# Another order of the experts' ranks in a mixture-of-experts layer, and each down projection loaded behind the next expert's gate and up

## The chip, the cores and the metric

The kernel runs on one core of a Trainium2 chip. The metric is the device time of one execution in microseconds (us); the median of several executions is compared.

## The reference

One decoder layer over 256 tokens of width 1024 in float32: a norm with modulation from a conditioning vector, a token mixer, and then a mixture of 64 experts, of which each token takes 8. The change touches the experts alone:

```python
def expert_block(args):
    x_b, g_b = args
    hg = jnp.einsum('td,edf->tef', x_b, w_gate)
    hu = jnp.einsum('td,edf->tef', x_b, w_up)
    return jnp.einsum('tef,efd->td', jax.nn.silu(hg) * hu * g_b[..., None], w_down)
```

`g_b` holds 8 gate values per token that aren't zero. `w_gate` and `w_up` are 1024 x 256 per expert and `w_down` is 256 x 1024, so each of the three matrices of an expert is 1 MiB.

## The kernel before

The first 260 us hold the norms, the token mixer, the router and a shared expert; the experts follow. At run time the experts are ranked by how many tokens they have. A unit is 32 tokens of one expert, and the table `UNITS` (line 32) fixes how many units each rank gets: 5 for ranks 0 and 1, 4 for rank 2, 3 for ranks 3 to 11, 2 for ranks 12 to 27, and 1 for ranks 28 to 48. `ORDER` (line 107) lists the ranks in the order in which they are worked. `plan_groups` (line 113) writes the units of the listed ranks one behind the other, after one unit for each of two experts loaded ahead of the ranking (ranks 64 and 65 in its lists), and cuts the list into 24 groups of 4 units, 128 token rows each. I number the groups from 0.

`run_groups` (line 1413) does a group in these steps, on TensorE in this order (helper `te`, line 1373, chains all of its matmuls, so they read L1378 in the profile): the gate and up products into the tile `pgu` (`pgum` in the profile), eight passes over the rows of the model width, and in each pass one matmul per part, a part being the neighbouring units that share an expert where `column_parts` (line 138) can merge them; the sums of the group before into `acc`; the gathering of token rows for later groups (`pgm`); transposes; and the down products (`pym`). In the first of the eight passes the matmul of each part needs its own expert's gate and up.

The weights arrive by transfers that SP issues from one queue, in program order. `load_experts` (line 1348) is called at the start of each group's code for the ranks that the group is the first to use. For each it takes the next pair of buffers from a ring of five (`wtiles`, line 1203; profile names gu, wbl, wbp for gate and up, and dn, wbs, wbd for down), reads the expert's number and issues gate, up and down, in this order:

```python
nc.sync.dma_start(out=gu[:, 0, :], in_=gsrc[ds(e * P, P), :], **kw)
nc.sync.dma_start(out=gu[:, 1, :], in_=usrc[ds(e * P, P), :], **kw)
late.append((dn, dsrc[ds(e * P, P), :], kw))
while late and not together:
    t, src, kw = late.pop()
    nc.sync.dma_start(out=t, in_=src, **kw)
```

A transfer into a buffer waits until TensorE has read what was in it for the last time, which was the expert five places earlier in the order; what is behind it in SP's queue waits too. In the last group (`together`) the down matrix is loaded in two halves by columns.

Of the kernel before, what the change touches and what calls it, by code (L numbers as in the profile page):

```python
# [17 lines left out]
SP = mybir.EngineType.SP  # L18

P = 128  # L20
T = 256
D = 1024
NE = 64
# [16 lines left out]
SKIPPABLE = 40  # L40
# [63 lines left out]

ORDER = [
    12, 0, 13, 28, 14, 29, 30, 15, 16, 3, 31, 17, 32, 33, 4, 34, 5, 35, 1, 18, 36, 19, 37, 38, 6, 39, 20, 21, 7, 40, 22, 41, 42,
    8, 43, 9, 44, 23, 24, 25, 45, 46, 10, 47, 11, 48, 26, 27, 2,
]  # L110


# [13 lines left out]
ULIST = [u for g in plan_groups() for u in g]  # L126
# [32 lines left out]
def tile_layer(ctx, tc, x, small, rows, w_ada, w_in, w_out, b_ada, gdn_norm_w, hg_norm_w, norm2_w, w_router, router_bias,  # L159
               w_gate, w_up, w_down, ws_gate, ws_up, ws_down, final_norm_w, consts, out, dbg=None):  # L160
# [999 lines left out]
    def glu(pgate, name):  # L1160

        sg = mo.tile([P, FE], F32, name=f"sg{name}", tag="sg", bufs=1)
        S.activation(sg, pgate[:, 0:FE], AF.Silu)  # L1163
        hh = mo.tile([P, 2, P], F32, name=f"hh{name}", tag="hh")
        V.tensor_tensor(hh.rearrange("p j q -> p q j"), sg.rearrange("p (q j) -> p q j", j=2),  # L1165
                        pgate[:, FE:2 * FE].rearrange("p (q j) -> p q j", j=2), op=ALU.mult)
        return hh
# [35 lines left out]
    def wtiles():  # L1203
        k = ring[0]
        ring[0] += 1
        return pairs[k % len(pairs)], downs[k % len(downs)]
# [138 lines left out]
    for b in range(2):  # L1345
        dense_down(hs[b], sdn, b, "sh", False)

    def load_experts(ranks, skippable, together):

        res, late = {}, []  # L1350
        for r in ranks:
            gu, dn = res[r] = wtiles()
            e = nc.values_load(order[0:1, r:r + 1], engines=[SP], min_val=0, max_val=NE - 1)
            kw = {}
            if skippable and r >= SKIPPABLE:
                n = nc.values_load(order[0:1, NE + r:NE + r + 1], engines=[SP], min_val=0, max_val=T)
                kw["cond"] = n > 0
            nc.sync.dma_start(out=gu[:, 0, :], in_=gsrc[ds(e * P, P), :], **kw)
            nc.sync.dma_start(out=gu[:, 1, :], in_=usrc[ds(e * P, P), :], **kw)
            late.append((dn, dsrc[ds(e * P, P), :], kw))  # L1360
            while late and not together:
                t, src, kw = late.pop()
                nc.sync.dma_start(out=t, in_=src, **kw)

        for n in range(2):
            for t, src, kw in late:
                t, src = (a.rearrange("p (j f) -> p j f", j=2)[:, :, n * 512:n * 512 + 512] for a in (t, src))
                nc.sync.dma_start(out=t, in_=src, **kw)
        return res

    last_pe = [None]

# [40 lines left out]
    def run_groups(u0, u1, prefix, skippable):  # L1413

        w = {NE + k: t for k, t in enumerate(ahead)}
        last_pe[0] = None
        groups = list(range(u0, u1, 4))
        starts = groups[::2]

        def batch(k):  # L1420
            return Batch(starts[k], min(8, u1 - starts[k]), f"{prefix}{starts[k]}")

        def scatter(n, st, yhl, name, first, stop):

            for k in range(2):
                for b in range(2):
                    te(TE.matmul, acc[b, n], lhsT=st[:, b, :], rhs=yhl[n][k], start=(first and k == 0), stop=(stop and k == 1), skip_group_check=True)

        before = None
        for k, u in enumerate(groups):  # L1430
            units = ULIST[u:u + 4]
            parts = column_parts([r for r, _ in units])
            name = f"{prefix}{u}"
            last = u + 4 == NMAIN
            new = [r for r in dict.fromkeys(r for r, _ in units) if r not in w]
            w.update(load_experts(new, skippable, last))
            if k == 0:
                nxt = batch(0)
                nxt.rows()
                for j2 in range(4):  # L1440
                    nxt.gather(j2)
            if k % 2 == 0:
                cur, nxt = nxt, None
                if k // 2 + 1 < len(starts):
                    nxt = batch(k // 2 + 1)
            o = P * (k % 2)
            if last:

                for n in range(2):
                    scatter(n, *before, False, True)  # L1450
                for n in range(2):
                    for b in range(2):
                        add_sums(b, n, name)

            pgu_ = pgu.tile([P, 512], F32, name=f"pgu{name}", tag="pgu")
            for j in range(8):
                for i, m, r in parts:
                    te(TE.matmul, pgu_[i:i + m, :], lhsT=cur.xg[j // 4][:, j % 4, o + i:o + i + m],
                       rhs=w[r][0][:, :, j * FE:j * FE + FE], start=(j == 0), stop=(j == 7))
            hh = glu(pgu_, name)  # L1460
            if before and not last:
                for n in range(2):
                    scatter(n, *before, not skippable and k == 1, False)

            ph = pht.tile([P, 512], F32, name=f"pht{name}", tag="pht")
            for b in range(2):
                te(TE.matmul, ph[:, 2 * P:2 * P + 8], lhsT=cur.sm[:, b, o:o + P], rhs=ghl[:, b, u // 4, :], start=(b == 0), stop=(b == 1))
            if nxt:
                if k % 2 == 0:
                    nxt.rows()  # L1470
                nxt.gather(2 * (k % 2))
            for j in range(2):
                te(TE.transpose, ph[:, j * P:j * P + P], hh[:, j, :], ident)
            hT_ = mo.tile([P, 2, P], F32, name=f"hTt{name}", tag="hTt")
            moved[0] = S.copy(hT_.rearrange("p j t -> p (j t)"), ph[:, 0:2 * P]).ins  # L1475
            gc = mo.tile([P, 1], F32, name=f"gc{name}", tag="gc")
            g4 = mo.tile([P, 8], F32, name=f"g4{name}", tag="g4")
            V.scalar_tensor_tensor(g4, ph[:, 2 * P:2 * P + 8], 1.0, blk4.rearrange("p k i -> p (k i)"), op0=ALU.mult, op1=ALU.mult, accum_out=gc)
            if nxt:
                nxt.gather(2 * (k % 2) + 1)  # L1480

            yhl = []
            for n in range(2):
                pyd = pg_.tile([P, 512], F32, name=f"py{name}{n}", tag="psg")
                for j in range(2):
                    for i, m, r in parts:
                        te(TE.matmul, pyd[i:i + m, :], lhsT=hT_[:, j, i:i + m],
                           rhs=w[r][1][:, j * D + n * 512:j * D + n * 512 + 512], start=(j == 0), stop=(j == 1))
                if last and n:
                    yh = mo.tile([P, 512], F32, name=f"yh{name}{n}", tag="yh")  # L1490
                    V.scalar_tensor_tensor(yh, pyd, gc, g2bc[:, n * 512:n * 512 + 512], op0=ALU.mult, op1=ALU.mult)
                    yhl.append((yh,))
                    continue
                yh, yl = (mo.tile([P, 512], F32R, name=f"y{c}{name}{n}", tag=f"y{c}") for c in "hl")
                if last:
                    y = mo.tile([P, 512], F32, name=f"y{name}{n}", tag="yd")
                    V.scalar_tensor_tensor(y, pyd, gc, g2bc[:, n * 512:n * 512 + 512], op0=ALU.mult, op1=ALU.mult)
                    S.copy(yh, y)
                    V.tensor_tensor(yl, y, yh.bitcast(F32), op=ALU.subtract)  # L1499
                else:  # L1500
                    S.activation(yh, pyd, AF.Copy, scale=gc)  # L1501
                    V.scalar_tensor_tensor(yl, pyd, gc, yh.bitcast(F32), op0=ALU.mult, op1=ALU.subtract)  # L1502
                yhl.append((yh, yl))
            before = cur.st[:, k % 2], yhl, name
        if not last:
            for n in range(2):
                scatter(n, *before, k == 0, True)
                for b in range(2):
                    add_sums(b, n, prefix)
            return  # L1510
        st, yhl, _ = before
        for n in range(2):
            sl = slice(n * 512, n * 512 + 512)
            for b in range(2):
                pso = acc[b, n]
                for k in range(2 - n):
                    te(TE.matmul, pso, lhsT=st[:, b, :].bitcast(F32) if n else st[:, b, :], rhs=yhl[n][k], start=(k == 0), stop=(k == 1 - n))
                V.tensor_tensor(x1[:, b, sl], x1[:, b, sl], pso, op=ALU.add)  # L1518
# [154 lines left out]
```

## Time and profile before

| | |
|---|---|
| median of 3 executions | 689.58 us (689.46 to 689.62) |
| the profiled execution, its own time | 688.26 us |
| span of its profile | 686.6 us |
| TensorE busy | 610.1 us, 89% of the span |
| VectorE / ScalarE / GpSimd busy | 301.3 / 209.6 / 121.7 us |
| bytes moved | 216.75 MB, mean 316 GB/s |
| mean granted TensorE clock | 0.953 |

The shares are means over stages. The expert stage is the stretch from about 260 us to 676 us; what a change there is worth has to be read from that stage's rows, and from what each engine waits for there.

### The profile page before, as it was taken

The page shows a single profiled execution, that of the slowest core. Times are in us where ns is not written, and L with a number is a line of the kernel's source. Part 1 is how long each engine was busy: PE and PEld are TensorE (multiplying, and loading weights), DVE is VectorE, ACT ScalarE, POOL GpSimd, SP SyncE. Part 2 cuts the span into 40 slices and gives each one's busy share as a digit, 9 for nine tenths or more (in the row PEclk, how much of TensorE's full clock was granted, in tenths as well). Part 3 has the DMA queues.
Part 4 walks back from the last instruction along what each step waited for, and adds up shares of the span by engine and source line. Part 5 has one row for each costly group of instructions (what it writes and reads, how often), then busy time and mean ns, then how long its engine had stood idle before and what let it go on. Part 6 is the DMA issues. An engine that isn't in the chain of part 4 may idle for free.

```text
span 686.6 us, 12745 instructions
## 1 busy us (share of the span) xinstructions
PE 610.1 (89%) x5161; PEld 379.2 (55%) x5162; DVE 301.3 (44%) x616; ACT 209.6 (31%) x410; POOL 121.7 (18%) x148
## 2 busy tenths in 40 slices
PE   4799887697889699999898899997998999799983
PEld 1499876586879687554443444543444444344441
DVE  4478999878998843122212022212121212121244
ACT  3356775433655321112111112111111111111113
POOL 7025273446566220000000000000000000000001
PEclk9899999889999879999999999998999999899998
DMA  8968383353665637796999999979999999999801
GB/s 350 421 275 313 138 330 127 125 200 156 262 243 217 263 137 298 314 376 244 408 426 420 422 422 422 423 259 420 424 422 424 420 425 420 425 416 425 348 0 66
DMA packets 31937, 216.75 MB, mean 316 GB/s; under 512 B 3760, under 2 KB 4096, under 8 KB 6400
## 3 DMA queue, kind: packets, MB, share of 16 engines
q1 hardware_dynamic: 31776, 215.83, 77.3%
q8 instruction: 42, 0.69, 0.4%
q14 instruction: 23, 0.19, 0.1%
q10 hardware_dynamic: 96, 0.04, 0.0%
HBM read 214.81 MB, written 1.05 MB: 314 GB/s over the span
## 4 chain that ended last, share of the span: by engine, by line
PE 61%; DMA 16%; DVE 16%; issue 3%; SPq 2%; ACT 2%; DVEq 0%; ACTq 0%
PE pgum L1378 21%; PE pym L1378 10%; PE acc L1378 6%; PE pgm L1378 5%; DMA wbl<-in_w_up_dram 5%; DMA gu<-in_w_up_dram 5%; DVE pacc L876 4%; PE pqk L437 3%; DMA ldA<-in_w_ada_dram 3%; PE pgs L1183 3%; DMA wbp<-in_w_up_dram 2%; DVE wps L451 2%; DVE cacc L541 2%; PE i L476 2%; PE gA L476 1%
## 5 line engine op out<-in xcount | busy, mean ns | idle before, releaser
L1378 PE MATMUL pgum<-wbl,xgm 128*32 128x512 f32 (+2 forms) x784 | 168.1, 629 | 6.6 <-DMA wbl<-in_w_up_dram 6.6
L1378 PE MATMUL pgum<-gu,xgm 128*32 128x512 f32 (+2 forms) x256 | 87.5, 606 | 7.5 <-DMA gu<-in_w_up_dram 7.5
L1378 PEld LDWEIGHTS pgum<-wbl,xgm 128*32 128x32 f32 (+2 forms) x784 | 47.5, 121 | 79.0 <-issue 79.0
L1165 DVE TENSOR_TENSOR hhm<-sgm,pgum 128x256 f32<-128x256 f32 x24 | 14.9, 621 | 172.1 <-ACT sgm L1163 172.1
L1378 PE MATMUL pgum<-wbp,xgm 128*32 128x512 f32 x224 | 78.0, 636 | 3.8 <-DMA wbp<-in_w_up_dram 3.8
L1536 POOL TENSOR_TENSOR o<-x_sb,fbc 128x512 f32<-128x512 f32 x2 | 2.5, 1269 | 418.1 <-DVE x_sb L1518 418.1
L1378 PE MATMUL pym<-wbs,hTtm 128*32 128x512 f32 (+1 forms) x272 | 72.6, 596 | 0.0
L1163 ACT ACTIVATE sgm<-pgum 128x256 f32<-128x256 f32 x24 | 9.2, 384 | 186.0 <-PE pgum L1378 186.0
L1502 DVE SCALAR_TENSOR_TENSOR ylm<-pym,gcm,yhm 128x512 fp32r<-128x512 f32 x46 | 34.6, 751 | 69.0 <-ACT yhm L1501 69.0
L1378 PE MATMUL pym<-wbd,hTtm 128*32 128x512 f32 (+2 forms) x232 | 61.7, 595 | 0.5 <-ACT hTtm L1475 0.5
L876 DVE SCALAR_TENSOR_TENSOR pacc<-ldc,cact,pacc 128x512 f32<-128x512 f32 x56 | 56.6, 1010 | 1.0
L1501 ACT ACTIVATE yhm<-pym,gcm 128x512 fp32r<-128x512 f32 x46 | 31.6, 687 | 76.1 <-PE pym L1378 76.1
L1378 PEld LDWEIGHTS pgum<-gu,xgm 128*32 128x32 f32 (+2 forms) x256 | 24.9, 126 | 46.0 <-issue 45.8
L1378 PE MATMUL pym<-dn,hTtm 128*32 128x512 f32 (+2 forms) x128 | 43.6, 596 | 0.5 <-ACT hTtm L1475 0.5
L1378 PE MATMUL pgm<-smm,h2hi 128*128 128x256 f32 x192 | 43.3, 305 | 0.0
L1378 PE MATMUL pgm<-smm,h2lo 128*128 128x256 f32 x192 | 38.5, 282 | 0.0
L1378 PE MATMUL acc<-yhm,stm 128*128 128x512 f32 x98 | 34.6, 434 | 0.0
L1378 PE MATMUL acc<-ylm,stm 128*128 128x512 f32 x94 | 29.8, 396 | 0.3 <-DVE ylm L1499 0.2
L1378 PEld LDWEIGHTS pgm<-smm,h2lo 128*128 128x128 f32 x192 | 29.6, 190 | 0.2 <-issue 0.2
L1378 PEld LDWEIGHTS pgm<-smm,h2hi 128*128 128x128 f32 x192 | 29.5, 190 | 0.3 <-issue 0.2
L1378 PEld LDWEIGHTS acc<-yhm,stm 128*128 128x128 f32 x98 | 16.7, 188 | 21.8 <-issue 18.9
L1378 PEld LDWEIGHTS pgum<-wbp,xgm 128*32 128x32 f32 x224 | 18.6, 116 | 16.3 <-issue 16.3
(454 smaller groups left out, 1082.4 us busy)
## 6 DMA issues: line engine op xcount, KB each, us to landing
wbl<-in_w_gate_dram SPq DMA_DIRECT2D x30, 1024.0 KB, 15.1
wbl<-in_w_up_dram SPq DMA_DIRECT2D x30, 1024.0 KB, 16.9
wbs<-in_w_down_dram SPq DMA_DIRECT2D x20, 1024.0 KB, 14.8
wbd<-in_w_down_dram SPq DMA_DIRECT2D x20, 1024.0 KB, 15.3
ldc<-in_w_ada_dram SPq DMA_DIRECT2D x16, 1024.0 KB, 7.9
gu<-in_w_gate_dram SPq DMA_DIRECT2D x11, 1024.0 KB, 15.1
gu<-in_w_up_dram SPq DMA_DIRECT2D x11, 1024.0 KB, 17.1
dn<-in_w_down_dram SPq DMA_DIRECT2D x10, 1024.0 KB, 15.4
```

The costliest lines, as they stand in the source:

```text
L437: TE.matmul(pqk[m // 2][:, (m % 2) * T:(m % 2) * T + T], lhsT=ws[j][PAIRS[k][0]][:, m * P:m * P + P], rhs=hT[:, PAIRS[k][1], j, :], start= ...
L451: engine(f"s_{key}{q}", "GGVG"[q]).tensor_tensor(lo, t[:, 2 * q:2 * q + 2, :], hi.bitcast(F32), op=ALU.subtract)
L476: TE.matmul(pj[:, i * T:i * T + T], lhsT=lh, rhs=rh, start=(i == 0 and j == 0 and k == 0), stop=(i == 1 and j == 7 and k == 2), skip_group ...
L541: V.scalar_tensor_tensor(acc, xp[:, k:k + T], convcol[:, 12 * k + blk:12 * k + blk + 1], acc, op0=ALU.mult, op1=ALU.add)
L876: engine(f"c{n}", "V").scalar_tensor_tensor(pa, t[:, :, j, :], cact[:, j:j + 1], pa, op0=ALU.mult, op1=ALU.add)
L1163: S.activation(sg, pgate[:, 0:FE], AF.Silu)
L1165: V.tensor_tensor(hh.rearrange("p j q -> p q j"), sg.rearrange("p (q j) -> p q j", j=2), pgate[:, FE:2 * FE].rearrange("p (q j) -> p q j", ...
L1183: TE.matmul(pg2[:, i * FE:i * FE + FE], lhsT=hT_all[j // 4][:, j % 4, b * P:b * P + P], rhs=gu[:, i, j * FE:j * FE + FE], start=(j == 0 an ...
L1378: last_pe[0] = fn(*args, **kw).ins
L1501: S.activation(yh, pyd, AF.Copy, scale=gc)
L1502: V.scalar_tensor_tensor(yl, pyd, gc, yh.bitcast(F32), op0=ALU.mult, op1=ALU.subtract)
L1536: G.tensor_tensor(o[b, n], x1[:, b, sl], fbc[:, sl], op=ALU.mult)
```

## The change

`ORDER` holds the same 49 ranks in another order, and the units of a rank stay together. `load_experts` becomes `load_gate`, which issues gate and up and puts the down load on the list `late`, and `load_downs(left)`, which issues from that list until `left` are on it. At the start of a group each new rank's gate and up is issued and then the downs but the newest one. After the group's gate and up products the gate and up of the first new rank of the next group are issued, and then the down that is left of this group. In the last group the downs of all ranks on the list come in halves at the end. Lines in the changed kernel stand one to eighteen lower.

```diff
 ORDER = [
-    12, 0, 13, 28, 14, 29, 30, 15, 16, 3, 31, 17, 32, 33, 4, 34, 5, 35, 1, 18, 36, 19, 37, 38, 6, 39, 20, 21, 7, 40, 22, 41, 42,
...
+    14, 12, 22, 19, 24, 15, 37, 11, 43, 13, 35, 18, 16, 6, 46, 8, 39, 4, 31, 10, 47, 1, 29, 23, 36, 38, 45, 0, 40, 32, 42, 7, 27,
...
-    def load_experts(ranks, skippable, together):
...
+    late = []
+
+    def load_gate(r, skippable):
+
+        gu, dn = wtiles()
+        e = nc.values_load(order[0:1, r:r + 1], engines=[SP], min_val=0, max_val=NE - 1)
...
+        nc.sync.dma_start(out=gu[:, 0, :], in_=gsrc[ds(e * P, P), :], **kw)
+        nc.sync.dma_start(out=gu[:, 1, :], in_=usrc[ds(e * P, P), :], **kw)
+        late.append((dn, dsrc[ds(e * P, P), :], kw))
+        return gu, dn
+
+    def load_downs(left, halves=False):
+
+        todo = [late.pop(0) for _ in range(max(len(late) - left, 0))]
+        if not halves:
+            for t, src, kw in todo:
                 nc.sync.dma_start(out=t, in_=src, **kw)
-
+            return
         for n in range(2):
-            for t, src, kw in late:
+            for t, src, kw in todo:
                 t, src = (a.rearrange("p (j f) -> p j f", j=2)[:, :, n * 512:n * 512 + 512] for a in (t, src))
                 nc.sync.dma_start(out=t, in_=src, **kw)
...
-            new = [r for r in dict.fromkeys(r for r, _ in units) if r not in w]
-            w.update(load_experts(new, skippable, last))
+            for r in dict.fromkeys(r for r, _ in units):
+                if r not in w:
+                    w[r] = load_gate(r, skippable)
+                    if not last:
+                        load_downs(1)
+            if last:
+                load_downs(0, True)
...
             hh = glu(pgu_, name)
+
+            ahead_ = 0
+            for r, _ in ULIST[u + 4:min(u + 8, u1)]:
+                if r not in w and not ahead_:
+                    w[r] = load_gate(r, skippable)
+                    ahead_ = 1
+            load_downs(ahead_)
```

From the two tables of ranks follow the groups. The number of ranks that each group, 0 to 23, is the first to use:

| | new ranks in groups 0 to 23 |
|---|---|
| before | 1 1 2 3 2 2 3 2 2 1 2 3 2 2 2 3 2 2 2 3 2 2 2 1 |
| changed | 1 2 2 3 2 2 2 2 2 2 2 1 3 2 2 2 2 2 2 2 2 2 2 3 |

Where the code moves instructions: SP's queue from the first expert loaded by rank, before. A name such as `wbl2` or `wbd0` is one buffer of the ring; only the transfers are shown.

```order
L1358 DMA wbp_2912<-in_w_gate_dram 128x2048
L1359 DMA wbp_2912<-in_w_up_dram 128x2048
...
L1363 DMA wbd0_2915<-in_w_down_dram 128x2048
...
L1358 DMA wbl2_2911<-in_w_gate_dram 128x2048
...
L1359 DMA wbl2_2911<-in_w_up_dram 128x2048
...
L1363 DMA wbd1_2916<-in_w_down_dram 128x2048
...
L1358 DMA wbl0_2909<-in_w_gate_dram 128x2048
...
L1359 DMA wbl0_2909<-in_w_up_dram 128x2048
...
L1363 DMA wbs0_2913<-in_w_down_dram 128x2048
...
L1358 DMA gu0_2704<-in_w_gate_dram 128x2048
```

The same place in the changed kernel:

```order
L1360 DMA wbp_2912<-in_w_gate_dram 128x2048
...
L1361 DMA wbp_2912<-in_w_up_dram 128x2048
...
L1360 DMA wbl2_2911<-in_w_gate_dram 128x2048
...
L1361 DMA wbl2_2911<-in_w_up_dram 128x2048
...
L1370 DMA wbd0_2915<-in_w_down_dram 128x2048
...
L1360 DMA wbl0_2909<-in_w_gate_dram 128x2048
...
L1361 DMA wbl0_2909<-in_w_up_dram 128x2048
...
L1370 DMA wbd1_2916<-in_w_down_dram 128x2048
...
L1360 DMA gu0_2704<-in_w_gate_dram 128x2048
...
L1361 DMA gu0_2704<-in_w_up_dram 128x2048
...
L1370 DMA wbs0_2913<-in_w_down_dram 128x2048
```

Each down has moved behind the gate and up of the next expert; the buffers go round the ring as before.

SP's queue at the end of the 24 groups, before:

```order
L1358 DMA wbl0_2909<-in_w_gate_dram 128x2048
...
L1359 DMA wbl0_2909<-in_w_up_dram 128x2048
...
L1363 DMA wbs0_2913<-in_w_down_dram 128x2048
...
L1358 DMA gu0_2704<-in_w_gate_dram 128x2048
...
L1359 DMA gu0_2704<-in_w_up_dram 128x2048
...
L1368 DMA dn0_2705<-in_w_down_dram 128x2x512
```

The same place in the changed kernel:

```order
L1360 DMA wbl0_2909<-in_w_gate_dram 128x2048
...
L1361 DMA wbl0_2909<-in_w_up_dram 128x2048
...
L1360 DMA gu0_2704<-in_w_gate_dram 128x2048
...
L1361 DMA gu0_2704<-in_w_up_dram 128x2048
...
L1375 DMA wbd1_2916<-in_w_down_dram 128x2x512
...
L1375 DMA wbs0_2913<-in_w_down_dram 128x2x512
...
L1375 DMA dn0_2705<-in_w_down_dram 128x2x512
```

The last group is now the first to use three experts instead of one, and their downs stand behind all gates and ups, in six half loads (the three shown, twice) instead of two.

## Rows read from the trace of the kernel before

**Rows 1.** Page, part 2: GB/s that the transfers moved, in 40 equal slices of the span
```profile
GB/s 350 421 275 313 138 330 127 125 200 156 262 243 217 263 137 298 314 376 244 408 426 420 422 422 422 423 259 420 424 422 424 420 425 420 425 416 425 348 0 66
```

**Rows 2.** Chain of waits, expert stage: start us, duration us, what it was
```profile
294.26 7.06 PE pgum L1378 x16
...
309.01 7.00 PE pgum L1378 x64
...
328.68 14.20 DMA gu<-in_w_up_dram
...
343.01 8.49 PE pgum L1378 x30
...
356.31 3.63 PE pym L1378 x16
...
380.52 8.48 PE pgum L1378 x58
...
442.23 7.00 PE pgum L1378 x64
...
477.06 9.70 PE pgum L1378 x58
...
495.14 7.02 PE pgum L1378 x32
...
529.18 8.72 PE pgum L1378 x58
...
561.12 6.87 PE pgum L1378 x64
...
596.20 9.87 PE pgum L1378 x58
```

**Rows 3.** Waits of TensorE for transfers, whole span: us in total, times, longest
```profile
PE pgum L1378 <- DMA gu<-in_w_up_dram: 7.5, 2, 4.8
PE pgum L1378 <- DMA wbl<-in_w_up_dram: 6.6, 2, 3.8
PE pgum L1378 <- DMA wbp<-in_w_up_dram: 3.8, 1, 3.8
```

**Rows 4.** Stretch: length; PE, PEld, DVE, ACT, POOL busy; clock, DMA share, GB/s
```profile
310.00:330.00 20.00, 20.00 (x178) 9.91 (x172) 3.58 (x7) 3.20 (x6) 0.00 (x0) 1.00 0.68 259
...
343.00:351.60 8.60, 8.59 (x31) 2.92 (x32) 0.00 (x0) 0.00 (x0) 0.00 (x0) 0.83 1.02 422
...
380.00:440.00 60.00, 59.48 (x422) 29.58 (x423) 11.98 (x26) 10.28 (x20) 0.00 (x0) 0.97 1.01 423
...
440.00:460.00 20.00, 20.00 (x158) 8.83 (x160) 4.49 (x8) 4.58 (x8) 0.00 (x0) 1.00 0.78 295
...
462.00:476.00 14.00, 11.30 (x90) 5.61 (x82) 3.75 (x8) 2.62 (x5) 0.00 (x0) 0.99 0.97 400
...
658.00:676.00 18.00, 16.19 (x44) 7.40 (x42) 10.33 (x18) 4.84 (x11) 1.24 (x2) 1.00 0.00 1
```

**Rows 5.** Timeline of SP's queue: start us, duration us of an issue, what
```profile
227.42 0.34 SPq L1141 DMA_DIRECT2D wbs<-in_ws_down_dram  x1
...
287.75 0.34 SPq L1358 DMA_DIRECT2D gu<-in_w_gate_dram  x1
...
316.03 0.34 SPq L1358 DMA_DIRECT2D wbl<-in_w_gate_dram  x1
...
324.41 0.33 SPq L1363 DMA_DIRECT2D wbd<-in_w_down_dram  x1
...
328.68 0.73 SPq L1359 DMA_DIRECT2D gu<-in_w_up_dram  x1
...
449.24 0.34 SPq L1358 DMA_DIRECT2D gu<-in_w_gate_dram  x1
```

**Rows 6.** DMA issues by line: KB each, median us from issue to landing
```profile
wbs<-in_ws_down_dram SPq DMA_DIRECT2D x1, 1024.0 KB, 4.9
```

**Rows 7.** Waits of SP's queue, whole span: us in total, times, longest
```profile
SPq L1363 <- PE pym L1378: 109.0, 19, 8.2
```

More of the change, by code (lines that the diff above doesn't have):

```diff
@@ L107 @@
 ORDER = [
-    12, 0, 13, 28, 14, 29, 30, 15, 16, 3, 31, 17, 32, 33, 4, 34, 5, 35, 1, 18, 36, 19, 37, 38, 6, 39, 20, 21, 7, 40, 22, 41, 42,
-    8, 43, 9, 44, 23, 24, 25, 45, 46, 10, 47, 11, 48, 26, 27, 2,
+    14, 12, 22, 19, 24, 15, 37, 11, 43, 13, 35, 18, 16, 6, 46, 8, 39, 4, 31, 10, 47, 1, 29, 23, 36, 38, 45, 0, 40, 32, 42, 7, 27,
+    26, 20, 5, 17, 3, 28, 25, 34, 2, 44, 30, 9, 41, 21, 33, 48,
 ]
@@ L1346, in tile_layer @@
         dense_down(hs[b], sdn, b, "sh", False)
-    def load_experts(ranks, skippable, together):
[L1350 to L1362, printed above, removed]
+    late = []
+    def load_gate(r, skippable):
+        gu, dn = wtiles()
+        e = nc.values_load(order[0:1, r:r + 1], engines=[SP], min_val=0, max_val=NE - 1)
+        kw = {}
+        if skippable and r >= SKIPPABLE:
+            n = nc.values_load(order[0:1, NE + r:NE + r + 1], engines=[SP], min_val=0, max_val=T)
+            kw["cond"] = n > 0
+        nc.sync.dma_start(out=gu[:, 0, :], in_=gsrc[ds(e * P, P), :], **kw)
[6 more added lines that the diff above has]
+            for t, src, kw in todo:
                 nc.sync.dma_start(out=t, in_=src, **kw)
+            return
         for n in range(2):
-            for t, src, kw in late:
+            for t, src, kw in todo:
                 t, src = (a.rearrange("p (j f) -> p j f", j=2)[:, :, n * 512:n * 512 + 512] for a in (t, src))
                 nc.sync.dma_start(out=t, in_=src, **kw)
-        return res
     last_pe = [None]
```

## The prediction

> **What bounds the kernel now.** I read the page's GB/s first. A slice is 686.6 / 40 = 17.2 us; from the 19th (309 us) to the 37th (652 us) nearly all show 408 to 426 GB/s, with dips at 244 and 259 and a last one of 348 [rows 1]. So the expert stage runs near the most that the transfers reach, and the busy share of TensorE, 89%, doesn't say alone which of the two sets the pace. The chain of waits says it [rows 2]. Most of it is TensorE, one group behind the other, and in between stand stretches in which the chain goes through a transfer of an up projection, as the one of 14.20 us that lands at 328.68 + 14.20 = 342.88. The list of waits confirms it: TensorE stands for transfers of ups five times, 7.5 + 6.6 + 3.8 = 17.9 us in all [rows 3]. No wait for a down stands in that list.
>
> Undisturbed, a group takes a steady time. From the end of gate and up in group 6 (380.52 + 8.48 = 389.00) to that in group 10 (442.23 + 7.00 = 449.23) it is 60.23 us, 15.06 each [rows 2]. The gate and up products take about 7.0 us whether they are one part (7.06, x16), two (7.02, x32) or four (7.00, x64) [rows 2].
>
> A wait costs more than its own length. Pairs of groups that hold one, between ends of gate and up, against 2 x 15.06 = 30.12 [rows 2]:
> - groups 3 and 4: 316.01 to 351.50 is 35.49, 5.4 too much;
> - 5 and 6: 351.50 to 389.00 is 37.50, 7.4;
> - 11 and 12: 449.23 to 486.76 is 37.53, 7.4;
> - 14 and 15: 502.16 to 537.90 is 35.74, 5.6;
> - 18 and 19: 567.99 to 606.07 is 38.08, 8.0.
>
> That is 33.7 us (the unrounded terms are 33.74), of which 17.9 is standing [rows 3]. The rest is mostly slow running afterwards: behind the wait that ends at 343.0 the granted clock is 0.83 over 8.6 us [rows 4], a mixture of the full 2.4 GHz and the lower 1.2 GHz, and gate and up takes 8.49 to 9.87 instead of 7.0 [rows 2].
>
> Why those groups? At full rate, 423 GB/s [rows 4], 1 MiB takes 1.0486 MB / 423 GB/s = 2.48 us, an expert 7.44 and two experts 14.87: just under a group's 15.06. A group that needs three new experts asks for 22.3 us of transfers. Groups 3, 6, 11, 15 and 19 need three, and every wait is in such a group or in the one behind it. The transfers also can't work far ahead. They stand idle in part from 310 to 330 us (259 GB/s) and from 440 to 460 (295) [rows 4]; against 423 that loses 20 x (1 - 259/423) = 7.8 and 6.1 us. These follow the two experts of five units. Rank 0 spreads over groups 1 and 2 and rank 1 over 9 and 10, and the loads that take their buffers are issued at 316.03 and 449.24 [rows 5], the moment their last gate and up product ends (316.01 and 449.23 [rows 2]), for use already in the next group. A down that waits for a down buffer holds up the gates behind it: SP's queue spends 109.0 us so [rows 7].
>
> **The change part by part.** No byte, unit or group is added: 49 experts, 24 groups. There are other parts per group, which costs nothing by the rows of one, two and four parts; the bounds are 0.06 x 24 = 1.4 us either way.
>
> The order. New experts per group are two, but for groups 0 and 11 (one) and 3, 12 and 23 (three), as front's table shows. No gate buffer is now wanted back with less than two groups between last and first use. I follow the ups against TensorE. Group 0's gate and up ends as before, and the first load that waits for it goes out at 287.75 [rows 5]. By the listing the next 14 transfers in the queue end with the up of rank 11, the eighth expert, which is the last that group 3 needs. None of the 14 has to wait beyond its turn: the latest-freed buffers come at 294.26 + 7.06 = 301.32, the end of group 1's gate and up [rows 2], and their transfers' turn comes after nine others, 287.75 + 9 x 2.48 = 310. From issue to landing there is an offset above the 2.48 per MiB: a lone load takes 4.9 [rows 6], so 2.4; the train of six that goes out from 324.41 [rows 5] lands at 342.88 [rows 2], 18.47 - 14.88 = 3.6. So the up lands at 287.75 + 14 x 2.48 + 2.4 to 3.6 = 324.9 to 326.1. Group 3 starts about one step after 309.01 [rows 2], at 324.1. TensorE waits 0.8 to 2.0 us; I take 1.5, nearer to the train, which is the more like case.
>
> From there each group with two new experts gains 15.06 - 14.87 = 0.19. The single one in group 11 gives 7.6, the three in group 12 take 7.3 back. Up to group 23 the supply needs 41 x 7.44 less the two downs that stand behind the last ups, 305.0 - 5.0 = 300.0, and TensorE 20 x 15.06 = 301.2. So no second wait, but with 0.2 to 3 us to spare in most groups.
>
> The downs. Each moves behind two transfers of the next expert, so a gate and up comes 2.48 us sooner and the down 4.96 later. A down is wanted only at 356.31 where gate and up ended at 351.50 [rows 2], 4.8 later, and some 12 us after the group's ups are wanted; that cover hides the 4.96. If it were gone, TensorE would wait in the down products instead. The downs' own waits for a buffer now stand behind a gate, which no longer waits for them.
>
> The tail. Group 23's downs are six halves, 3 x 2.48 = 7.4 us behind the last up; their products come 7.0 + 4.8 = 11.8 behind. Hidden, nothing added. Four more issues on SP, at 0.33 us each [rows 5], lie in a queue that runs ahead.
>
> The clock after the one wait that is left. The shortest wait with a slow stretch behind it, 2.7 us (7.5 less 4.8 [rows 3]), made 5.4 - 2.7 = 2.7 of slow running; from 658 to 676 TensorE was idle for 18.00 - 16.19 = 1.8 us in pieces and kept a clock of 1.00 [rows 4]. So 0 to 2.7; I take 0, as 1.5 us is nearest to the latter. The Trainium skill, TensorE: Matmul & The Clock Gate, section "HAM oscillation — how this bites in real kernels", says that compute pieces with waits for the next slice between them start cold again each time; the clock of 0.83 behind the waits agrees [rows 4]. By that rule the wait in group 3 costs its slow stretch too and the time would be 2.7 us longer, 660.0.
>
> The sum, for the profiled execution: 688.26 - 33.7 + 1.5 + 0 = 656.0. That execution lies 689.58 - 688.26 = 1.3 below the median, so **657.3 us** on the median's scale. With no wait and no offset it would be 654.5.
>
> **The rivals.**
> A, the transfers become the pace: with so little to spare, a rate slightly lower makes every group wait. From 462 to 476 it was 400 GB/s [rows 4]; at that, two experts take 15.73, 0.67 more than a step, and 20 groups lose 13.4: 671. For it: the thin margin. Against it: 422 or 423 GB/s in the longer stretches [rows 4], at the same queue depth.
>
> B, the waits stay where three experts are new: groups 3, 12 and 23 at the mean of the five, 33.7 / 5 = 6.7, make 20.2 us: 688.3 - 33.7 + 20.2 + 1.3 = 676. Against it: group 12 follows the group with one, and in 23 two downs stand behind.
>
> C, slower: a down is now stuck behind the next gate, and if that gate's buffer comes free only with the current group's gate and up, the down goes out then, with two transfers ahead of it, and lands 2.4 + 3 x 2.48 = 9.8 later, 5.0 after it is wanted (4.8). It decides from the point where more than 33.7 / 5.0 = 7 groups do this; over 20 groups it would be 100 us, 689.6 - 33.7 + 100 = 756. Against it: the ring's next buffer belongs to an expert last used two groups back or more.
>
> D, the order doesn't matter: the same bytes at 423 GB/s, and what is gained early is lost at the end, 689.6. Against it: 13.9 us of idle transfers in two stretches, with waits of TensorE right behind both.
>
> **How the numbers follow.** The forecast gets 0.74, A 0.11, B 0.07, C 0.05, D 0.03. 0.2% of the time, 1.4 us, is about what a measurement tells from no change; forecast, A and B are faster by far more, so faster 0.92, same 0.03, slower 0.05. The range goes from 654.5, the sum without any wait, to 668, which holds one or two waits with their slow stretches (5.4 to 8.0) and the milder half of A.
>
> **What would show it.** Right: the gate and up products stay near 7.0 us in all groups but perhaps group 3; the waits of TensorE for ups fall from 17.9 to about 1.5 us; steps stay at 15.06; GB/s has no dip after 290 us and the last load lands near 636 us; the granted clock stays at 1.00. Wrong: a new wait of TensorE's down products for a dn, wbs or wbd transfer (C), ups waited for in many groups by under a microsecond each (A), or five-microsecond waits at groups 3, 12 and 23 (B).

## The result, and the profile after

| | before | changed |
|---|---|---|
| median | 689.52 us (688.41 to 689.62, 4 runs) | 659.29 us (658.64 to 660.42, 4 runs) |
| the profiled execution, its span | 688.26, 686.6 us | 658.64, 656.9 us |

The ratio is 0.9567, with a 95% interval of 0.9549 to 0.9585: 4.3% faster. The forecast was 657.3 us, 2.0 too low.

The page's GB/s of the changed kernel, 40 slices of 16.4 us, answers to [rows 1]:

```profile
GB/s 346 421 327 287 149 287 121 235 102 160 266 181 391 77 370 82 313 307 422 424 421 425 419 428 422 421 421 421 426 421 424 420 424 423 422 424 421 424 263 69
```

From the 19th slice to the 38th no dip is left. The stretch from 310 to 330 us, which stood at 259 GB/s [rows 4], is full now, and so are the 330 us from 290 on (same columns as there: stretch, length, five engines' busy times, clock, DMA share, GB/s):

```profile
310.00:330.00 20.00, 19.54 (x126) 8.55 (x126) 2.98 (x6) 3.21 (x6) 0.00 (x0) 1.00 1.01 423
...
290.00:620.00 330.00, 329.54 (x2507) 156.68 (x2500) 72.87 (x150) 62.69 (x118) 0.00 (x0) 1.00 1.01 423
```

TensorE is busy 329.54 of the 330 us from 290 to 620, at a clock of 1.00. Its waits for ups, in the list that answers to [rows 3] (us in total, times, longest):

```profile
PE pgum L1384 <- DMA gu<-in_w_up_dram: 1.7, 1, 1.7
...
PE pgum L1384 <- DMA wbl<-in_w_up_dram: 0.5, 1, 0.5
```

They were 17.9 us in five. The chain of waits, answering to [rows 2] (start us, duration, what), shows where the two stand:

```profile
279.71 7.00 PE pgum L1384 x64
...
304.19 20.71 DMA wbl<-in_w_up_dram
324.95 7.05 PE pgum L1384 x58
...
339.99 6.99 PE pgum L1384 x64
...
581.40 6.87 PE pgum L1384 x64
...
609.95 19.95 DMA gu<-in_w_up_dram
...
630.03 7.04 PE pgum L1384 x58
```

The first is in group 3, the second in group 23. Between them a step is still what it was: the gate and up products of groups 4 and 20 start at 339.99 and 581.40, (581.40 - 339.99) / 16 = 15.09 us.

One number serves for all comparisons below, the length of the expert stage: from the start of group 0's gate and up to the end of group 23's. It leaves out the earlier stages, in which executions differ by some microseconds. Before it is 660.11 + 6.88 - 280.74 = 386.25 us, changed 630.03 + 7.04 - 279.71 = 357.36. The two rows of before, from its chain of waits:

```profile
280.74 7.00 PE pgum L1378 x64
...
660.11 6.88 PE pgum L1378 x16
```

So 28.9 of the 29.6 us by which the two profiled executions differ lie in this stage.

### The profile page after: what moved, and what is told of

Its sections match the earlier page's. It is cut to its first block, busy times and chain, and to the rows that moved or that the text cites. A ratio compares the mean times of both kernels' runs of the same rounds, so it can differ in the third digit from the quotient of the medians.

```text
span 656.9 us, 13082 instructions
## 1 busy us (share of the span) xinstructions
PE 596.5 (91%) x5329; PEld 371.8 (57%) x5330; DVE 301.0 (46%) x616; ACT 209.9 (32%) x410; POOL 121.5 (18%) x148
## 4 chain that ended last, share of the span: by engine, by line
PE 61%; DVE 17%; DMA 16%; issue 3%; ACT 2%; SPq 0%; DVEq 0%; ACTq 0%
PE pgum L1384 21%; PE pym L1384 10%; PE acc L1384 6%; PE pgm L1384 6%; DVE pacc L877 4%; DMA ldA<-in_w_ada_dram 3%; DMA wbl<-in_w_up_dram 3%; DMA gu<-in_w_up_dram 3%; PE pqk L438 3%; DMA wbp<-in_w_up_dram 3%; PE pgs L1184 3%; DVE wps L452 2%; DVE cacc L542 2%; DMA dn<-in_w_down_dram 2%; DMA ldwo<-in_w_out_dram 2%
## 5 line engine op out<-in xcount | busy, mean ns | idle before, releaser
L1384 PE MATMUL pgum<-wbl,xgm 128*32 128x512 f32 (+1 forms) x928 | 170.6, 593 | 0.5 <-DMA wbl<-in_w_up_dram 0.5
L1384 PEld LDWEIGHTS pgum<-wbl,xgm 128*32 128x32 f32 (+1 forms) x928 | 49.8, 113 | 76.2 <-issue 74.2
L1384 PE MATMUL pgum<-gu,xgm 128*32 128x512 f32 (+1 forms) x208 | 84.5, 593 | 1.7 <-DMA gu<-in_w_up_dram 1.7
L1384 PE MATMUL pgum<-wbp,xgm 128*32 128x512 f32 (+1 forms) x240 | 84.7, 593 | 0.0
L1384 PE MATMUL pym<-wbs,hTtm 128*32 128x512 f32 (+1 forms) x288 | 83.5, 596 | 0.5 <-ACT hTtm L1493 0.5
L1384 PE MATMUL pym<-wbd,hTtm 128*32 128x512 f32 (+1 forms) x296 | 61.7, 595 | 0.5 <-ACT hTtm L1493 0.5
L1384 PE MATMUL pym<-dn,hTtm 128*32 128x512 f32 (+1 forms) x104 | 43.5, 596 | 0.0
L1384 PEld LDWEIGHTS pgum<-gu,xgm 128*32 128x32 f32 (+1 forms) x208 | 22.1, 116 | 25.1 <-issue 25.0
L1384 PEld LDWEIGHTS pym<-wbs,hTtm 128*32 128x32 f32 (+1 forms) x288 | 20.2, 113 | 21.6 <-issue 19.5
L1384 PEld LDWEIGHTS pgum<-wbp,xgm 128*32 128x32 f32 (+1 forms) x240 | 21.4, 112 | 15.4 <-issue 15.4
L1384 PEld LDWEIGHTS pgm<-smm,h2lo 128*128 128x128 f32 x192 | 29.6, 190 | 0.2 <-issue 0.2
## 6 DMA issues: line engine op xcount, KB each, us to landing
wbl<-in_w_gate_dram SPq DMA_DIRECT2D x30, 1024.0 KB, 16.4
gu<-in_w_gate_dram SPq DMA_DIRECT2D x11, 1024.0 KB, 16.4
```

The costliest lines, as they stand in the source:

```text
L1384: last_pe[0] = fn(*args, **kw).ins
```

## The experiments

The theory: groups that ask for three new experts, and transfers that pause for want of buffers, made the waits; the order of ranks spreads the demand, and that is most of the gain. The rival: it's the place of the downs, which lets the gates and ups run ahead. Medians of before are those of the same chip; the last two columns come from the profiled execution. "Listed" is the sum of the waits for ups that stand in the list for TensorE's matmuls of gate and up.

| run | median us | before us | ratio, 95% interval | stage us | listed us |
|---|---|---|---|---|---|
| order alone | 660.78 | 688.53 | 0.9608, 0.9566 to 0.9650 | 358.17 | 2.4 |
| loads alone | 679.13 | 688.53 | 0.9865, 0.9822 to 0.9909 | 377.17 | 14.6 |
| first downs earlier | 655.61 | 688.53 | 0.9528, 0.9493 to 0.9562 | 354.92 | 0.9 |
| no gate ahead | 656.81 | 688.53 | 0.9533, 0.9495 to 0.9571 | 354.85 | 0.8 |
| changed, again | 658.19 | 688.24 | 0.9565, 0.9540 to 0.9591 | 357.34 | 2.2 |
| before, light downs | 661.78 | 688.24 | 0.9625, 0.9597 to 0.9653 | 358.71 | 2.6 |
| changed, light downs | 655.54 | 688.24 | 0.9525, 0.9494 to 0.9556 | 353.85 | 0 |
| three new in group 6 | 665.84 | 688.24 | 0.9686, 0.9656 to 0.9715 | 364.49 | 6.5 |
| changed, beside | 658.85 | 688.20 | 0.9579, 0.9554 to 0.9604 | 357.43 | 2.2 |
| first downs earlier, beside | 656.53 | 688.20 | 0.9529, 0.9509 to 0.9549 | 354.85 | 0.8 |
| no gate ahead, beside | 657.71 | 688.20 | 0.9554, 0.9535 to 0.9572 | 354.79 | 0.8 |

The changed kernel was also run again by itself. It was expected at a ratio of 0.955 to 0.959, with a wait of half a microsecond in group 3 and one of 1.7 in group 23; it came at 0.9565 with 0.6 and 1.6.

**Order alone, loads alone.** The first is the kernel before with the new `ORDER`, the second the changed kernel with the old one:

```diff
-ORDER = [12, 0, 13, 28, 14, 29, 30, 15, 16, 3, 31, 17, 32, 33,
...
+ORDER = [14, 12, 22, 19, 24, 15, 37, 11, 43, 13, 35, 18, 16, 6,
```

> The new order of ranks with the old way of loading (gate, up, down of each expert together, all at the start of its group). Theory (the order spreads the transfers evenly, and that is nearly the whole gain): four or five of the five waits are gone, but the up that group 3 waits for lands some 2.5 us later than with the late downs, so a wait of about 4 us with a slow clock behind it stays there: 661 to 664 us, ratio 0.958 to 0.963. Rival (the late downs make most of the gain): the waits stay in number, 675 us or more, ratio above 0.978.

> The old order with the new way of loading (downs behind the next expert's gate and up, one gate and up ahead of its group). Theory (the order is the gain): the groups with three new experts still ask for 22 us of transfers in 15; the waits of groups 4 and 12 become small, those of groups 6, 15 and 19 stay with 5 to 7 us each: 678 to 684 us, ratio 0.983 to 0.992. Rival (the late downs make most of the gain): under 670 us, ratio below 0.972.

Both came nearly as the theory had them; the median with the order alone is 0.2 us below its range. With the order alone one wait is left, in group 3 (list of waits, and the chain's gate and up behind it):

```profile
PE pgum L1378 <- DMA wbl<-in_w_up_dram: 2.4, 1, 2.4
...
327.59 8.72 PE pgum L1378 x58
```

With the loads alone three are left, in groups 6, 15 and 19, those with three new experts (two of them 5.4 and 5.9 us as expected, that of group 19 only 8.7 - 5.4 = 3.3); the waits of groups 4 and 12, right behind such a group, are gone:

```profile
PE pgum L1384 <- DMA wbl<-in_w_up_dram: 8.7, 2, 5.4
...
PE pgum L1384 <- DMA gu<-in_w_up_dram: 5.9, 1, 5.9
```

By the stage, the order alone saves 386.25 - 358.17 = 28.1 us and the loads alone 9.1; together they save 28.9. So of the change's two halves the order makes nearly all, and on top of it the new place of the downs adds 0.8 us. That 0.8 is the difference of two larger terms. Group 3's gate and up takes 8.6 us instead of the 12.2 with the order alone (from 324.14 to 327.59 + 8.72 = 336.31), 3.6 less. But TensorE then comes earlier to group 23, where with the order alone it didn't wait, and loses 2.8 there.

How long SP stands at a buffer doesn't tell what TensorE loses. With the order alone SP's wait for down buffers is longer than the 109.0 us of before [rows 7], though the stage is 28 us shorter:

```profile
SPq L1363 <- PE pym L1378: 134.2, 21, 7.8
```

**Three new experts in one group.** One exchange in the changed kernel's order makes group 6 the first to use three experts and group 19 only one:

```diff
-    14, 12, 22, 19, 24, 15, 37, 11, 43, 13, 35, 18, 16, 6, 46,
+    14, 12, 22, 19, 24, 15, 37, 11, 43, 13, 35, 18, 28, 34, 6, 46,
...
-    26, 20, 5, 17, 3, 28, 25, 34, 2, 44, 30,
+    26, 20, 5, 17, 3, 16, 25, 2, 44, 30,
```

> The changed kernel with one exchange in the order: rank 16 (two units) trades places with ranks 28 and 34 (one unit each), so that group 6 is the first to use three experts and group 19 only one; bytes, units and groups are the same. Theory (with no slack in hand, a group that asks for a third expert waits for its 7.4 us less the little that is saved, and the clock falls behind the wait): a wait of 5 to 6 us in group 6 and a slow stretch of 2.5 to 3, while the wait in group 23 goes because TensorE is then later: 664 to 668 us, 5 to 9 above the changed kernel, ratio 0.963 to 0.970. Rival (the number of new experts of a single group doesn't matter, the late downs cover it): within 2 us of the changed kernel.

The list, the chain, and the stretch of group 6's gate and up:

```profile
PE pgum L1384 <- DMA wbl<-in_w_up_dram: 6.5, 2, 6.0
```

```profile
377.43 9.77 PE pgum L1384 x60
```

```profile
374.00:385.00 11.00, 7.57 (x48) 2.23 (x52) 0.00 (x0) 0.00 (x0) 0.00 (x0) 0.69 1.01 422
```

A wait of 6.0 us came in group 6 where it was expected, with the slow stretch behind it (9.77 instead of 7.0, mean clock 0.69), and none in group 23. The stage is 7.1 us longer than the changed kernel's, with the same bytes, units and number of transfers. One more thing is different in it: the third expert of group 6 takes a buffer that group 5 is the last to use, so SP issues its gate only at 362.63, when group 5's gate and up ends (355.75 + 6.96 = 362.71). That isn't what made the wait, for the transfers were busy with what stood ahead of it in the queue all the time:

```profile
355.00:375.00 20.00, 16.43 (x136) 7.16 (x128) 5.08 (x10) 3.31 (x6) 0.00 (x0) 1.00 1.01 422
```

So the third expert's bytes made it, as the theory had it.

**Lighter downs.** Only half of each down matrix is loaded from the seventh expert on (the sixth in the changed kernel, where downs are issued one expert later; the last group's are whole), in both kernels (of the computation, the down products then use what an earlier load left in the other half of the buffer; the work of the engines is the same):

```diff
+                m = 2048 if ring[0] < 10 else 1024
-                nc.sync.dma_start(out=t, in_=src, **kw)
+                nc.sync.dma_start(out=t[:, 0:m], in_=src[:, 0:m], **kw)
```

> The kernel before with lighter transfers: from the seventh expert loaded by rank on, only the first half of each down matrix is loaded (the products run on what is in the buffer, so TensorE's work is the same), 2.5 MiB an expert instead of 3. Theory (the five waits come from too many bytes asked for in a short time, and cost 33.7 us with their slow clock): an expert takes 6.2 us, three take 18.6 against a step of 15.06, and nearly all waits go without any change of order: 656 to 662 us, ratio 0.951 to 0.960. Rival (the waits come from buffers that come free too late, which fewer bytes don't mend): at least two waits stay, 670 us or more, ratio above 0.971.

> The changed kernel with the same lighter downs. Theory (TensorE sets the pace and the transfers are only just behind it): the wait in group 23 goes, 2.8 us, and that in group 3 mostly stays, since most downs ahead of it are still whole: 655 to 657 us, ratio 0.950 to 0.953. Rival (the transfers set the pace of the changed kernel): the expert stage shortens with the bytes, by tens of microseconds: under 640 us, ratio below 0.93.

In the kernel before, fewer bytes do most of what the order does: the stage falls by 27.5 us. Two short waits are left (1.5 and 1.1 us), so the ratio ended a little above what was expected, between theory and rival but far nearer to the theory: two waits stay, as the rival had it, but at a median of 661.78 us and not at 670. The two are in groups 12 and 4, whose gate and up takes about 2.5 and 2.2 us longer than 7.05 (461.01 to 470.56 and 337.29 to 346.54):

```profile
339.49 7.05 PE pgum L1379 x30
...
463.53 7.03 PE pgum L1379 x58
```

Both come behind the experts with five units, where the transfers still pause in this kernel, down to

```profile
435.00:440.00 5.00, 5.00 (x38) 2.39 (x30) 0.62 (x1) 0.38 (x1) 0.00 (x0) 1.00 0.14 31
```

That speaks for the buffers as the cause of some 4.7 of the 6 us that are left, though no run freed those buffers alone. In the changed kernel the wait of group 23 went, and of group 3's loss half stayed, 0.8 us: it is not among the listed waits, but gate and up takes from 325.81 to 325.88 + 7.77 = 333.65, 7.84 instead of 7.05. The stage fell by 3.5 us to 353.85, no further, though its transfers had bytes to spare: TensorE's own 24 groups are the bound below that.

**The head.** Two variants of the changed kernel. In one the newest down is issued before the gate ahead in the first two groups:

```diff
             ahead_ = 0
+            if u < 8:
+                load_downs(0)
             for r, _ in ULIST[u + 4:min(u + 8, u1)]:
```

> The changed kernel, but in its first two groups the down of the newest expert is issued before the next gate and up, so that one more down goes out before the queue stands at the buffer that group 0 frees. Theory (from then on the transfers run without a pause, so what is 2.5 us earlier at group 3 is 2.5 us earlier at group 23 as well): the waits in both groups go, 1.5 and 2.8 us: 655 to 656 us, ratio 0.950 to 0.952. Rival (the wait in group 23 belongs to the three experts of the last group alone): only group 3's goes, 657.5 to 658, ratio about 0.954.

In the other no gate is issued ahead of its group:

```diff
-            ahead_ = 0
-            for r, _ in ULIST[u + 4:min(u + 8, u1)]:
-                if r not in w and not ahead_:
-                    w[r] = load_gate(r, skippable)
-                    ahead_ = 1
-            load_downs(ahead_)
+            load_downs(0)
```

> The changed kernel without the gate and up of the next group's first expert issued ahead: at the end of each group's gate and up products all downs on the list are issued, so only the downs within a group stand behind a gate. Theory (the order is the gain, and a down has some 12 us of cover): no new wait for a gate; the down that is issued before group 0's buffer comes free also helps as in the run with the early downs: 655 to 659 us, ratio 0.950 to 0.956. Rival (issuing ahead is what keeps the transfers from pausing): pauses in GB/s after 300 us and waits for ups, 665 us or more, ratio above 0.965.

SP's queue shows what moved. In the changed kernel, its timeline with the down for `wbs` behind the gate and up that wait for group 0 (start us, duration of the issue, what):

```profile
286.72 0.34 SPq L1360 DMA_DIRECT2D gu<-in_w_gate_dram  x1
...
287.78 0.33 SPq L1370 DMA_DIRECT2D wbs<-in_w_down_dram  x1
```

and in the variant with the first downs earlier:

```profile
275.20 0.33 SPq L1370 DMA_DIRECT2D wbs<-in_w_down_dram  x1
...
284.54 0.34 SPq L1360 DMA_DIRECT2D gu<-in_w_gate_dram  x1
```

The down goes out 9.3 us before the gate instead of 1.1 us behind it. So it is loaded ahead of the pause at the head and no longer behind it; the pause in the changed kernel:

```profile
284.00:286.00 2.00, 2.00 (x24) 0.61 (x20) 0.00 (x0) 0.00 (x0) 0.00 (x0) 1.00 0.00 0
```

The wait of group 3 goes and that of group 23 falls from 1.7 to 0.9 us; the stage loses 357.36 - 354.92 = 2.4 us, the time of one transfer of 1 MiB. So the wait of group 23 isn't the last group's own; it hangs on when the uninterrupted run of transfers began. It had been expected to go altogether, and it didn't. The variant with no gate ahead does the same by the stage, 354.85: after the head nothing is gained by issuing ahead.

Since these two had run on another chip than the repeat of the changed kernel, both ran again beside it:

> The changed kernel, beside the two runs with earlier downs on the same chip: ratio 0.955 to 0.959.

> The version with the first downs earlier, beside the changed kernel on the same chip. Theory (one MiB earlier at the head is 2.5 us earlier at the end): 2 to 3 us below the changed kernel, ratio lower by 0.003 to 0.005. Rival (the difference between the two calls was the chips'): within 0.5 us.

> The version without the gate and up ahead of its group, beside the changed kernel on the same chip. Theory: the same as the version with the first downs earlier, within 0.7 us, since its first downs go out early as well and nothing after that waits for them. Rival (the gate ahead saves something later on): no lower than the changed kernel.

The version with the first downs earlier is 2.3 us below the changed kernel (656.53 against 658.85), ratios 0.9529 and 0.9579; their intervals just don't overlap. The one with no gate ahead is 1.1 us below, and its interval (0.9535 to 0.9572) overlaps both; by the stage, 354.79 and 354.85, the two variants are the same, so its median's lag of 1.2 us, more than the 0.7 expected, lies outside the expert stage as far as the profiled executions show it. Of the kernels that load all weights, the one with the first downs earlier has the lowest median, by a margin over the one with no gate ahead that the intervals don't settle.

## Why the prediction was right, and where it was off

**The 33.7 us of waits and slow clock**, the main term, held. Without them the old stage would be 386.25 - 33.74 = 352.5; the changed kernel with lighter downs has 353.85, of which 0.8 is what it still loses in group 3.

**The wait of group 3**, taken as 1.5 us, was 1.6: its first products begin at 323.43 and its last end at 324.95 + 7.05 = 332.00, 8.57 instead of 7.0. The list shows 0.5 of it, because the parts that have their weights run on alone for a while before TensorE stands.

**The clock behind it**, taken as unharmed, was unharmed: 1.00 from 324.9 to 332.0. The Trainium skill, TensorE: Matmul & The Clock Gate, section "HAM oscillation — how this bites in real kernels", tells of slow starts in a kernel that waits some 3 to 5 us ahead of each piece, so the prediction stretched it when it applied it to a wait of 1.5. In these runs listed waits of 0.4 to 1.8 us left the clock at 1.00; those of 2.4 us and more were followed by 8.45 to 9.87 us instead of 7.0. How slow it became didn't go with the wait: 5.9 us with the loads alone were followed by 8.53, 3.8 in the kernel before by 9.70. The price of 2.7 us was too high besides. Of the 5.4 us of groups 3 and 4, 2.7 is the listed wait and 8.49 - 7.0 = 1.5 slow running; the rest is mostly the 1.1 us of products that ran alone ahead of the wait (they begin at 339.26).

**Between groups 4 and 22** no wait came, as forecast, with steps of 15.09 against 15.06. Rivals A and B are out for the middle: no group but 3 and 23 waits, and group 12 with its three new experts passes. In B's other two groups, 3 and 23, TensorE does lose time, but 1.6 and 2.8 us and not B's 6.7. Rival C found no place: no wait for a down is listed. SP's time at downs that wait for TensorE fell, in the list that answers to [rows 7], from 109.0 us to 52.6. But the prediction's gate, "which no longer waits for them", waits for gate buffers instead (before, then changed):

```profile
SPq L1358 <- PE pgum L1378: 77.5, 18, 16.0
...
SPq L1370 <- PE pym L1384: 52.6, 16, 4.8
...
SPq L1360 <- PE pgum L1384: 112.0, 21, 15.1
```

Together they are 186.5 us before and 164.6 changed: SP stands nearly as long as before, while the transfers have no pause left after the 18th slice.

Rival D fell with the result.

**The step that failed** is the one on the supply up to group 23: "Up to group 23 the supply needs 41 x 7.44 less the two downs that stand behind the last ups, 305.0 - 5.0 = 300.0". From the up of rank 11, which lands at 304.19 + 20.71 = 324.90, to that of rank 48 at 609.95 + 19.95 = 629.90, it took 305.0 us, and TensorE had to wait for the last. Two things were wrong. The count is one short: in SP's queue stand the gates and ups of 41 experts and 40 downs between those two, 122 transfers and not 121, because three downs (not two) stand behind the last up and two older ones come in at the front. At the forecast's own 423 GB/s that makes 302.4 us, 1.2 more than TensorE's 301.2; counted right, the forecast would have had a second wait. And the 122 landed in 2.50 us each instead of 2.48, which is the other 2.6. TensorE's own 20 steps, from the end of group 3's gate and up to that of group 23 without its wait, took 637.07 - 2.8 - 332.00 = 302.3 instead of 301.2, 1.1 more. So 1.2 + 2.6 - 1.1 = 2.7 us became a loss. The timeline of TensorE in group 23:

```profile
627.27 1.06 PE L1384 MATMUL pgum<-wbl,xgm 128*32 128x512 f32 x6
630.03 0.59 PE L1384 MATMUL pgum<-gu,xgm 128*32 128x512 f32 x1 [1.71 <-DMA gu<-in_w_up_dram]
```

From 627.27 to 630.03 + 7.04 = 637.07 it is 9.80 instead of 7.0: 2.8 us. The milder side of rival A, then, at a place where it wasn't looked for.

**The balance** of the profiled execution: 656.0 was forecast, 658.64 measured. The wait of group 23 adds 2.8 and that of group 3 0.1 more than taken; the stage's other steps make 357.36 - 352.51 - 1.6 - 2.8 = 0.45, and the stages outside it were 0.7 shorter (688.26 - 386.25 = 302.0, now 658.64 - 357.36 = 301.3): 656.0 + 2.8 + 0.1 + 0.45 - 0.7 = 658.65. The last step, 1.3 us from the profiled execution to the median, was 659.29 - 658.64 = 0.65 this time.

**The head.** The prediction told that downs move behind gates and costed their delay at nothing, with the cover in front of the down products. That held for the downs. But at the head a down that was ready stood behind a gate that had to wait for a buffer, while the transfers ran dry, and what was lost there came back as waits: with that down issued first, group 3's 1.5 us went and group 23's loss fell by 0.8. This 2.4 us was in the forecast's landing times and not recognised as a cost of the change.

## What to carry to other kernels

Where loading and computing take nearly the same time per step (14.87 and 15.06 us here), look at how many bytes each step asks for first, not at the mean: spreading the demand was worth 28 us of 386, and three experts instead of two in a single group cost 7. A short wait costs more than it shows, by the parts that run alone ahead of it and, for the waits of 2.4 us and more here, by the clock behind it. And in a queue that works in order, put what can go now ahead of what must wait for a buffer, above all before a long run of transfers without a pause.

## What the runs showed of the hardware that I had not expected

The landings came a little behind the bytes. Over 330 us the transfers moved 423 GB/s, by which 122 MiB (127.9 MB) take 302.4 us; the last of them landed after 305.0, 0.9% more. A small part is that the 423 counts the engines' other transfers too (the page lists 0.91 MB of instructions in the whole span). At the end, when only the half downs were left and nothing new was issued, the 16 engines didn't finish together:

```profile
632.00:634.00 2.00, 2.00 (x24) 0.73 (x20) 0.00 (x0) 0.00 (x0) 0.00 (x0) 1.00 0.77 291
634.00:636.00 2.00, 2.00 (x24) 0.63 (x17) 0.00 (x0) 0.00 (x0) 0.00 (x0) 1.00 0.53 205
636.00:638.00 2.00, 1.38 (x8) 0.41 (x3) 0.42 (x1) 0.38 (x1) 0.00 (x0) 1.00 0.15 55
```

Their mean busy share falls from 0.77 over 0.53 to 0.15 within six microseconds. A transfer that waits for its slowest engine while the others already work on later ones would land late in just this way. The trace doesn't tell the engines apart here, and no run tested it, so that reading stays open.
